# Ten more seven-product pairs in the second feed-forward, with their weight sums made in the mixers and kept in DRAM

## The chip, the cores and the metric

The kernel runs on one core of one Trainium2 chip. The metric is the device time in microseconds. The kernel before took 2288.7 us, the median of three runs (2288.67 to 2288.89).

## The reference

One layer of a decoder on 256 tokens of 2048 features, all in fp32: a gated feed-forward, two mixers of tokens side by side, a second gated feed-forward, and a gated embedding, each followed by a layer norm. Cut to what matters here:

```python
def swiglu(x, w_gu, w_down):
    g, u = jnp.split(x @ w_gu, 2, axis=-1)
    return (jax.nn.silu(g) * u) @ w_down

h = layer_norm(alpha * h + 0.5 * swiglu(h, w_ffn1_gu, w_ffn1_down), ...)   # f1
... # retention and sliding-window attention, gated, mixed                  # the mixers
h = layer_norm(alpha * h + mixed, ...)
h = layer_norm(alpha * h + 0.5 * swiglu(h, w_ffn2_gu, w_ffn2_down), ...)   # f2
ple = jax.nn.sigmoid(h @ w_ple_gate) * (p @ w_ple_proj)
h = layer_norm(alpha * h + ple, ...)
```

The change touches the product `x @ w_gu` of the second feed-forward: 256 x 2048 by 2048 x 11264.

## The kernel before

**Products.** Each fp32 operand is split into a high part (a copy to fp32r) and a low part (what the copy lost), and a product is three matmuls: low times high, high times high, high times low (`Sum.add`, lines 300 to 302). Weights come from HBM in chunks of 512 KB (`Chunk`, 128 partitions x 2 x 512 elements); for each, ACT makes the high part (`split`, line 93) and DVE the low one (line 94).

**Blocks.** The gate-and-up product of a feed-forward is done in eleven blocks (`for j in range(KF // 4)` in `ffn`), each of 512 columns of the gate and 512 of the up part. A block goes through eight pairs of 128-row slices of the weights, in an order written out as a string (`gu_units`, line 724). A letter P is a plain pair: two units `Single`, one for the gate and one for the up chunk, with 2 slices x 2 halves of the tokens x 3 = 12 matmuls each, 24 in all. A letter S is a `Seven` (line 142): Strassen's scheme, in Winograd's form, for the 2 x 2 block product of (two halves of the tokens, two slices) by (two slices, gate and up). It takes seven products for eight, 21 matmuls, and needs sums: of the activations (`seven_forms`, line 364, made once per feed-forward), and of the weights. For each seven DVE makes the four weight sums t1 to t4 (lines 165 to 168) in two tiles `u` and `v` of 128 x 1024, ACT and DVE split both, and they split the raw chunks too, as far as they are used. Block 0 has plain pairs alone; odd blocks have three sevens (`PPSPSPSP`, slices' pairs 0 to 2), even ones four (`PPSSPSSP`, pairs 0 to 3). At the end of a block's last seven, `seven_common` (line 401) and lines 825 to 830 join the sums; two units into the next block PE transposes the result (line 776).

**Order.** The program is written in the order in which each engine takes its instructions; an engine waits only for data and for room. Weight units stand in one list, `plan`, for the whole kernel. After each unit `done` calls `fill` (line 186): it issues the loads of further units on SP's queue while less than `far` (90) units of time are loaded or made, and has ACT and DVE split them while less than `ahead` (45) are made; a unit's time is 12 for a Single and 21 for a Seven, which is its matmuls. Both are held back by a budget, `slots_for_weights(n)`, of tiles of 4 KB a partition; a unit has `loads` (tiles that its load takes), `makes` (further ones while it is made) and `keeps` (those it holds until its matmuls are done). In f2 the budget is 24 from block 0 on. The tiles come from one pool of 46 (`SLOTS`), which holds activations too. A load whose tile is not free yet makes SP wait, with all that is queued behind it.

**Beside the matmuls.** `run_side` (line 236) is called after each unit. It takes one job from the list `side` (attention, transposes) and moves the first generator of the list `lazy` one step. The only generators are the tables of rotary angles, `rotary_table`: a DMA on ACT's queue, some twenty operations of 128 x 256 on DVE and two on ACT, in a dozen steps. The table for attention, "a", enters the list after the eight groups of queries and keys (`rqk`, until about 826 us), so it is made beside the three blocks of values (`rv`) that follow. After these come the retention's gates (`rg`), the attention's features (`av`, `aqk`), the two output gates (`gt`, `ga`), the output projections (`ma`, `mr`) and the mixing (`mo`). In the queries' and keys' stage, and at the attention's features, POOL multiplies by the angles (lines 931 to 933).

Of the kernel before, what the change touches and what calls it, by code (L numbers as in the profile page):

```python
# [8 lines left out]
F32 = mybir.dt.float32  # L9
F32R = mybir.dt.float32r  # L10
# [5 lines left out]
P = 128  # L16
# [20 lines left out]


SEVEN = (0, 1, 2, 3)

SEVEN_DOWN = (6, 7, 8, 9)

# [8 lines left out]
def layer(ctx: ExitStack, tc: tile.TileContext, io):  # L51
# [90 lines left out]
    class Seven:  # L142
# [12 lines left out]
        def make(self):  # L155
            a, b = self.a, self.b
            nm = a.name
            b11, b21, b12, b22 = a.of(a.raw, 0), a.of(a.raw, 1), b.of(b.raw, 0), b.of(b.raw, 1)
            u, v = (slot([P, 2, 512], F32, w + nm) for w in "uv")

            def shaped(x):
                return x.rearrange("p (g n) -> p g n", g=2) if a.paired else x

            t1, t3, t2, t4 = (shaped(x) for x in (u[:, 0], u[:, 1], v[:, 0], v[:, 1]))
            dve.tensor_tensor(t1, b11, b12, ALU.add)
            dve.tensor_tensor(t3, b12, b22, ALU.add)  # L166
            dve.tensor_tensor(t2, b11, t3, ALU.add)
# [12 lines left out]
            self.t1, self.t3 = parted("u", u)  # L180
            self.t2, self.t4 = parted("v", v)

    loaded, ready = [], []
    room = {"slots": 0, "used": 0, "ahead": 45, "far": 90, "quiet": False}
# [137 lines left out]
    def block_units(units, keys):  # L322

        for kind, p in units:
            if kind == "P":
                plan.extend(Single(keys(n, p)) for n in range(2))
            else:
                plan.append(Seven(keys(0, p), keys(1, p)))

    def block(name, units, keys, lhs, forms, sums, fold, before=None):  # L330


        sevens = [p for kind, p in units if kind == "S"]
        if sevens:
            p1, p6, p7, q5 = (Sum(bank(f"{name}s{j}"), len(sevens)) for j in range(4))
        for j, (kind, p) in enumerate(units):
            if before is not None:
                before(j)
            if kind == "P":
                for n in range(2):  # L340
                    u = take(keys(n, p))
                    tokens_chunk(u.chunk, 2 * p, lhs, [sums[t][n] for t in range(2)], (0, 1))
                    done(u)
                    run_side()
                continue
            u = take(keys(0, p))
            a11, a12 = (half_of(lhs(2 * p + e), 0) for e in range(2))
            a22 = half_of(lhs(2 * p + 1), 1)
            f5, f6, f7, f3 = forms(p)
            q2, q3, q4 = sums[0][0], sums[0][1], sums[1][0]  # L350
            steps = [
                (p1, a11, u.b11), (q2, a12, u.b21), (q3, f3, u.b22), (q5, f5, u.t1),
                (p7, f7, u.t3), (p6, f6, u.t2), (q4, a22, u.t4),
            ]
            if p == sevens[-1]:
                steps = [steps[j] for j in (0, 3, 5, 4, 1, 2, 6)]
            for to, left, right in steps:
# [32 lines left out]
    def units_of(order, sevens):  # L390

        sevens = list(sevens)
        plain = [p for p in range(KD // 2) if p not in sevens]
        return [(kind, (sevens if kind == "S" else plain).pop(0)) for kind in order]

    def block_sums(ps, units, n_k):

# [323 lines left out]
        yield  # L721


    def gu_units(j):
        if j == 0:
            return [("P", p) for p in range(KD // 2)]
        order = "PPSSPSSP" if j % 2 == 0 else "PPSPSPSP"
        return units_of(order, SEVEN[: order.count("S")])

# [19 lines left out]

    def plan_ffn(name):  # L750
        for j in range(KF // 4):
            block_units(gu_units(j), gu_keys(name, j))
        first, second, held = down_units(HELD_PAIRS[name == "f2"])
        block_units(first, down_keys(name, 0))
        block_units(second, down_keys(name, 1))
        plan.extend(Single(down_keys(name, 1)(n, p)) for n in range(2) for p in held)

    def ffn(name, i, ht, norm, keep, residual, keepers, away):
# [27 lines left out]

        for j in range(KF // 4):
            pg, pu = banks(f"{name}g{j}"), banks(f"{name}u{j}")
            units = gu_units(j)
            plain = len(units) - sum(kind == "S" for kind, p in units)  # L790
            n_of = {(0, 0): KD, (0, 1): KD, (1, 0): KD, (1, 1): KD}
            for kind, p in units:
                if kind == "S":
                    for at in ((0, 0), (0, 1), (1, 0)):
                        n_of[at] -= 1
                    n_of[1, 1] -= 2
            sums = [[Sum((pg, pu)[n][t], n_of[t, n]) for n in range(2)] for t in range(2)]
            got = []

            if norm is not None and j == 0:  # L800
                front, units = units[:FRONT_PAIRS], units[FRONT_PAIRS:]
                steps = [(gu_keys(name, 0)(n, p), 2 * p, n) for _, p in front for n in range(2)]
                norm.first(steps, rhs, sums, (
                    (3, (1, 0)), (5, (1, 1)), (7, (0, 2)), (8, (1, 2)), (9, (0, 3)), (10, (1, 3)), (10, "go"),
                ))
                slots_for_weights(24)

            def before(u, j=j, offset=KD // 2 - len(units)):
                u += offset
                if j == 0 and norm is None and u % 2 == 0:  # L810
                    first_chunk(u // 2)
                    if u == 6:
                        slots_for_weights(24)
                    if u == 2:
                        load_constants()
                if j == 0 and u == 7:
                    for g in sorted({p // 2 for p in SEVEN}):
                        hi, lo = (slot([P, 8, P], F32R, f"{name}f{w}{g}") for w in "hl")
                        made[g] = seven_forms(keep[g], hi, lo)
                if j == KF // 4 - 1 and u in (4, 6):  # L820
                    convert(u // 2 - 2)

            block(f"{name}{j}", units, gu_keys(name, j), rhs, forms, sums, lambda *a: got.extend(seven_common(*a)), before)
            if got:
                g, v = got
                for x, ps in ((g, pg), (v, pu)):
                    for t in range(2):
                        dve.tensor_tensor(x[:, t], x[:, t], ps[t], ALU.add)  # L828
                act.activation(g, g, AF.Silu)  # L829
# [141 lines left out]
    def mixers(ht, norm, residual, keepers, away):  # L971
# [27 lines left out]
            done(u)  # L999
        values(0, ps)  # L1000
        slots_for_weights(14)
        for grp in range(8):
            ps = banks(f"rqk{grp}")
            features_out([(("w_in_f", grp), ps)], KD, both_halves)
            rotated(grp, ps)
        grp = 8
        decay = [slot([P, 2, 384], F32, f"dec{j}") for j in range(4)]
        for j in range(4):
            act.dma_start(decay[j], io["decay"][:, 2 * j : 2 * j + 2, :])
        lazy.append(rotary_table("a"))  # L1010
        for blk in range(1, 4):
            ps = banks(f"rv{blk}")
            tokens_out(("w_rv", blk), KD, rhs, ps)
# [290 lines left out]

        lhs = lambda k: of_pairs(mix_t, k)
        slots_for_weights(16)
        for blk in range(3):
            if blk == 2:
                load_for_norm(1)
            ps = banks(f"mo{blk}")  # L1310
            y[blk] = load_columns(residual, blk, "mixy")
            tokens_out(("w_mix", blk), KD, lhs, ps)
            for t in range(2):
                dve.scalar_tensor_tensor(y[blk][:, t], y[blk][:, t], ALPHA, ps[t], ALU.mult, ALU.add)
            block_stats(stats, y, blk)
# [307 lines left out]
```

## Time and profile before

| | |
|---|---|
| Median of three runs | 2288.7 us |
| The profiled execution's own time | 2289.47 us |
| Its span, first to last instruction | 2287.7 us |
| Mean granted TensorE clock | 0.999 |
| DVE, busy share of the span | 85% |
| ACT, busy share of the span | 52% |
| DMA traffic | 465.88 MB, 204 GB/s on average |
| HBM read, written | 455.60 MB, 8.39 MB |

The kernel's stages by the trace: f1's gate and up to about 520 us, its second product to 690, the mixers to 1480, f2's gate and up to 1956, its second product to 2155, then the embedding. A stretch of the windows view gives its length and then, for PE, PEld (weight loads), DVE, ACT and POOL, the busy time with the number of instructions, and last the granted clock, the DMAs' busy share and GB/s. A line of the tile view gives the smallest, median and largest duration of an instruction in ns, the first and last start, and the shape. Busy time of PE overlaps from one matmul to the next, so the length of a stretch divided by its matmuls tells more than a matmul's duration.

### The profile page before, as it was taken

To read this page: it belongs to the slowest core of one execution; us is meant where nothing else is said; L and a number is where in the kernel's file an instruction comes from. 1 tells how busy PE (TensorE), PEld (TensorE's weight loads), DVE (VectorE), ACT (ScalarE), POOL (GpSimd) and SP (SyncE) were. 2 spreads that over 40 slices of the span, in tenths; PEclk is the share of its full clock that TensorE was granted. 3 is DMA by queue.
4 is the path that set the end of the run, shared out by engine and by line. 5 is a ranking of instruction groups with operands and counts; after the bars stand their busy time and mean duration, and the time that the engine had idled before them with its cause. 6 is when DMAs were issued, how large, how long until landed. Compare 5 with 4: busy or idle time off the path is not lost.

```text
span 2287.7 us, 28860 instructions
## 1 busy us (share of the span) xinstructions
PE 2271.4 (99%) x10490; PEld 1884.8 (82%) x10490; DVE 1947.8 (85%) x2474; ACT 1190.0 (52%) x1438; POOL 97.0 (4%) x56
## 2 busy tenths in 40 slices
PE   9999999999999999999999999999999999999998
PEld 7888888888888888888778888888888888888876
DVE  7899999999988785677789786779999999889877
ACT  6555555556554342435556454355565555555533
POOL 0000000000000530124000000000000000000000
PEclk9999999999999999999999999999999999999999
DMA  8666665655677565555447567566666566565772
GB/s 298 202 204 199 197 210 180 207 198 191 217 278 279 178 221 167 167 165 165 139 149 244 168 222 275 192 233 205 195 191 205 184 203 214 181 221 193 276 258 74
DMA packets 194022, 465.88 MB, mean 204 GB/s; under 512 B 14796, under 2 KB 16460, under 8 KB 193880
## 3 DMA queue, kind: packets, MB, share of 16 engines
q1 hardware_dynamic: 191752, 461.20, 61.0%
q10 hardware_dynamic: 2128, 2.84, 0.4%
q8 instruction: 82, 1.34, 0.2%
q14 instruction: 60, 0.49, 0.1%
HBM read 455.60 MB, written 8.39 MB: 203 GB/s over the span
## 4 chain that ended last, share of the span: by engine, by line
PE 95%; DVE 3%; DMA 1%; issue 0%; ACT 0%; DVEq 0%; ACTq 0%
PE f1g L300 3%; PE f1g L301 3%; PE f1g L302 3%; PE f2g L302 3%; PE f2g L300 3%; PE f2g L301 3%; PE rqk L251 3%; PE f1u L302 2%; PE f1u L301 2%; PE f1u L300 2%; PE f2u L302 2%; PE f2u L300 2%; PE f2u L301 2%; PE aqk L251 2%; PE f1d L300 2%; PE f2d L301 2%
## 5 line engine op out<-in xcount | busy, mean ns | idle before, releaser
L94 DVE TENSOR_TENSOR lf_gu<-rf_gu,hf_gu 128x1024 fp32r<-128x1024 f32 (+1 forms) x284 | 334.3, 1210 | 15.1 <-ACT hf_gu L93 14.3
L93 ACT CAST hf_gu<-rf_gu 128x1024 fp32r<-128x1024 f32 (+1 forms) x284 | 282.3, 1043 | 19.6 <-DMA rf_gu<-in_f_gu 19.4
L94 DVE TENSOR_TENSOR lw_in_f<-rw_in_f,hw_in_f 128x1024 fp32r<-128x1024 f32 x140 | 195.6, 1427 | 29.5 <-ACT hw_in_f L93 26.9
L94 DVE TENSOR_TENSOR lf_down<-rf_down,hf_down 128x1024 fp32r<-128x1024 f32 x152 | 181.1, 1219 | 22.7 <-ACT hf_down L93 20.2
L93 ACT CAST hf_down<-rf_down 128x1024 fp32r<-128x1024 f32 x152 | 155.2, 1050 | 74.8 <-DMA rf_down<-in_f_down 21.2
L93 ACT CAST huf_gu<-uf_gu 128x1024 fp32r<-128x1024 f32 x70 | 73.7, 1053 | 157.8 <-DVE uf_gu L166 155.2
L93 ACT CAST hw_in_f<-rw_in_f 128x1024 fp32r<-128x1024 f32 x140 | 138.9, 1051 | 2.2 <-DMA rw_in_f<-in_w_in_f 1.1
L300 PE MATMUL f1g<-hf_gu,xt 128*128 128x512 f32 x247 | 97.0, 393 | 0.8 <-ACT hf_gu L93 0.8
L301 PE MATMUL f1g<-hf_gu,xt 128*128 128x512 f32 x247 | 96.8, 392 | 0.0
L302 PE MATMUL f1g<-lf_gu,xt 128*128 128x512 f32 x247 | 96.7, 391 | 0.0
L300 PE MATMUL f2g<-hf_gu,ht 128*128 128x512 f32 x247 | 96.3, 390 | 0.0
L302 PE MATMUL f2g<-lf_gu,ht 128*128 128x512 f32 x247 | 96.2, 389 | 0.0
L301 PE MATMUL f2g<-hf_gu,ht 128*128 128x512 f32 x247 | 96.1, 389 | 0.0
L93 ACT CAST hvf_gu<-vf_gu 128x1024 fp32r<-128x1024 f32 x70 | 73.8, 1054 | 29.7 <-DVE vf_gu L168 29.4
L829 ACT ACTIVATE eve<-eve 128x1024 f32<-128x1024 f32 x20 | 21.2, 1061 | 124.4 <-DVE eve L828 124.4
L94 DVE TENSOR_TENSOR luf_gu<-uf_gu,huf_gu 128x1024 fp32r<-128x1024 f32 x70 | 85.2, 1217 | 0.0
L94 DVE TENSOR_TENSOR lvf_gu<-vf_gu,hvf_gu 128x1024 fp32r<-128x1024 f32 x70 | 85.2, 1217 | 0.0
L300 PE MATMUL f2u<-hf_gu,ht 128*128 128x512 f32 x212 | 83.8, 395 | 0.0
L300 PE MATMUL f1u<-hf_gu,xt 128*128 128x512 f32 x212 | 83.4, 393 | 0.0
L302 PE MATMUL f2u<-lf_gu,ht 128*128 128x512 f32 x212 | 82.6, 390 | 0.0
L301 PE MATMUL f2u<-hf_gu,ht 128*128 128x512 f32 x212 | 82.6, 390 | 0.0
L301 PE MATMUL f1u<-hf_gu,xt 128*128 128x512 f32 x212 | 82.6, 389 | 0.0
(1358 smaller groups left out, 6446.2 us busy)
## 6 DMA issues: line engine op xcount, KB each, us to landing
rf_gu<-in_f_gu SPq DMA_DIRECT2D x350, 512.0 KB
rf_down<-in_f_down SPq DMA_DIRECT2D x176, 512.0 KB
rw_in_f<-in_w_in_f SPq DMA_DIRECT2D x148, 512.0 KB
rw_rv<-in_w_rv SPq DMA_DIRECT2D x32, 512.0 KB
rw_ret<-in_w_ret SPq DMA_DIRECT2D x32, 512.0 KB
rw_mix<-in_w_mix SPq DMA_DIRECT2D x32, 512.0 KB
rw_pg<-in_w_pg SPq DMA_DIRECT2D x32, 512.0 KB
rw_att<-in_w_att SPq DMA_DIRECT2D x16, 512.0 KB
```

Of the source, the lines that this page charges most:

```text
L93: act.copy(dst_hi, src)
L94: (lo_engine or dve).tensor_tensor(dst_lo, src, dst_hi, ALU.subtract)
L251: pe.matmul(ps[f], hi[:, kk, f * P : (f + 1) * P], rhs(k), start=k == 0, stop=k == n_k - 1,)
L300: pe.matmul(o, al, bh, start=first, stop=False)
L301: pe.matmul(o, ah, bh, start=False, stop=False)
L302: pe.matmul(o, ah, bl, start=False, stop=self.left == 0)
L829: act.activation(g, g, AF.Silu)
```

## The change

In f2's blocks 1, 3, 5, 7 and 9 two plain pairs (pairs 4 and 5) become units of a new kind, D (`Prepared`): the order is `PPSDSDSP`. A D unit does the same seven products, and its four weight sums are not made on the spot. Its load brings the gate chunk (512 KB), that half of the up chunk which is used by itself (256 KB), and the high and low parts of `u` and `v` (four times 512 KB) from DRAM, six loads in all; the making of it splits the first two alone.

The sums and their parts are made in the mixers by `sums_ahead`, a generator of the list `lazy`. For each of the ten pairs it loads the two raw chunks, adds and splits, and stores the four parts in DRAM, 2 MB, in four pieces with pauses of `every` steps between them. Three pairs are made at a pause of 2, three at 3 and two at 5, from the values' blocks on; the last two, at 2, in the mixing. The next pair's raw chunks are loaded in the middle of a pair. The table of the attention's angles moves ahead of the queries' and keys' groups.

In f2's block 0 the sums of activations for pairs 4 and 5 are made as well (`forms_of`: one add of 128 x 1024, four of 128 x 256, one split). The budget of tiles becomes 32 - j at the start of each of the five blocks (31, 29, 27, 25, 23), and stays so in the block after it.

```diff
+AHEAD = (4, 5)
+AHEAD_BLOCKS = (1, 3, 5, 7, 9)
+AHEAD_SLOTS = 32
...
+    class Prepared:
+        loads, makes, keeps, time = 6, 3, 7, 21
...
+        def load(self):
+            self.a = Chunk(self.key)
+            self.b = slot([P, 2, 256], F32, "r" + self.a.name + "b")
+            sync.dma_start(self.b, chunk_of(self.other)[:, :, 256:])
+            self.sums = []
+            for w, v in zip(("hu", "lu", "hv", "lv"), put_by_sums.pop(self.key)):
+                t = slot([P, 2, 512], F32R, w + self.a.name)
+                sync.dma_start(t.bitcast(F32), v)
+                self.sums.append(t)
+
+        def make(self):
+            a = self.a
+            a.make()
+            self.b11, self.b21 = a.columns(0), a.columns(1)
+            both = slot([P, 2, 512], F32R, "b" + a.name)
+            self.b22 = both[:, 0], both[:, 1]
+            split(*(both[:, e].rearrange("p (g n) -> p g n", g=2) for e in range(2)), self.b)
...
+    def sums_ahead(items, wait, every):
...
+        pairs = [[Chunk(k) for k in items[0]]]
+        for _ in range(wait):
+            yield
+        for j, (key, _) in enumerate(items):
...
+            dve.tensor_tensor(t1, b11, b12, ALU.add)
+            dve.tensor_tensor(t3, b12, b22, ALU.add)
+            act.copy(uh, u)
+            yield from pause()
+            dve.tensor_tensor(t2, b11, t3, ALU.add)
+            dve.tensor_tensor(t4, t2, b21, ALU.add)
+            act.copy(vh, v)
+            if j + 1 < len(items):
+                pairs.append([Chunk(k) for k in items[j + 1]])
+            yield from pause()
+            dve.tensor_tensor(ul, u, uh, ALU.subtract)
+            yield from pause()
+            dve.tensor_tensor(vl, v, vh, ALU.subtract)
+            for e in range(2):
+                sync.dma_start(away[e], parts[e].bitcast(F32))
+            yield from pause()
+            for e in range(2, 4):
+                sync.dma_start(away[e], parts[e].bitcast(F32))
...
-    def gu_units(j):
+    def gu_units(name, j):
         if j == 0:
             return [("P", p) for p in range(KD // 2)]
+        if name == "f2" and j in AHEAD_BLOCKS:
+            return units_of("PPSDSDSP", SEVEN[:3], AHEAD)
...
                         made[g] = seven_forms(keep[g], hi, lo)
+                    if name == "f2":
+                        g = AHEAD[0] // 2
+                        made[g] = forms_of([ht[:, 4 * g : 4 * g + 4, :]], f"{name}f{g}")
+                if name == "f2" and j in AHEAD_BLOCKS and u == 0:
+                    slots_for_weights(AHEAD_SLOTS - j)
...
         slots_for_weights(14)
+        lazy.append(rotary_table("a"))
         for grp in range(8):
...
-        lazy.append(rotary_table("a"))
+        ahead = [(gu_keys("f2", j)(0, p), gu_keys("f2", j)(1, p)) for j in AHEAD_BLOCKS for p in AHEAD]
+        for items, every in ((ahead[:3], 2), (ahead[3:6], 3), (ahead[6:8], 5)):
+            lazy.append(sums_ahead(items, 3, every))
         for blk in range(1, 4):
...
         slots_for_weights(16)
+        lazy.append(sums_ahead(ahead[8:], 4, 2))
         for blk in range(3):
```

More of the change, by code (lines that the diff above doesn't have):

```diff
@@ L181, in make, with __init__ @@
             self.t2, self.t4 = parted("v", v)
+    put_by_sums = {}
+    class Prepared:
+        loads, makes, keeps, time = 6, 3, 7, 21
+        def __init__(self, key, other):
+            self.key, self.other = key, other
+        def load(self):
[14 more added lines that the diff above has]
+            split(*(both[:, e].rearrange("p (g n) -> p g n", g=2) for e in range(2)), self.b)
+            uh, ul, vh, vl = self.sums
+            self.t1, self.t3 = ((uh[:, e], ul[:, e]) for e in range(2))
+            self.t2, self.t4 = ((vh[:, e], vl[:, e]) for e in range(2))
@@ new lines, in sums_ahead, with pause @@
+    def sums_ahead(items, wait, every):
+        def pause():
+            for _ in range(every):
+                yield
+        pairs = [[Chunk(k) for k in items[0]]]
+        for _ in range(wait):
+            yield
+        for j, (key, _) in enumerate(items):
+            a, b = pairs.pop()
+            b11, b21, b12, b22 = a.of(a.raw, 0), a.of(a.raw, 1), b.of(b.raw, 0), b.of(b.raw, 1)
+            u, v = (slot([P, 2, 512], F32, w + a.name) for w in "uv")
+            t1, t3, t2, t4 = (x.rearrange("p (g n) -> p g n", g=2) for x in (u[:, 0], u[:, 1], v[:, 0], v[:, 1]))
+            parts = [slot([P, 2, 512], F32R, w + a.name) for w in ("hu", "lu", "hv", "lv")]
+            uh, ul, vh, vl = parts
+            away = [dram.tile([P, 2, 512], F32, name=f"{w}{a.name}") for w in ("hud", "lud", "hvd", "lvd")]
+            put_by_sums[key] = away
+            dve.tensor_tensor(t1, b11, b12, ALU.add)
[16 more added lines that the diff above has]
+                sync.dma_start(away[e], parts[e].bitcast(F32))
@@ L327, in block_units @@
             else:
-                plan.append(Seven(keys(0, p), keys(1, p)))
+                plan.append((Seven if kind == "S" else Prepared)(keys(0, p), keys(1, p)))
     def block(name, units, keys, lhs, forms, sums, fold, before=None):
-        sevens = [p for kind, p in units if kind == "S"]
+        sevens = [p for kind, p in units if kind != "P"]
         if sevens:
@@ L388, in forms_of, with units_of @@
         return seven_forms(whole(parts, name + "w"), hi, lo)
[L390 to L394, printed above, removed]
+    def units_of(order, sevens, ahead=()):
+        sevens, ahead = list(sevens), list(ahead)
+        plain = [p for p in range(KD // 2) if p not in sevens + ahead]
+        of = {"S": sevens, "D": ahead, "P": plain}
+        return [(kind, of[kind].pop(0)) for kind in order]
     def block_sums(ps, units, n_k):
@@ L751, in plan_ffn @@
         for j in range(KF // 4):
-            block_units(gu_units(j), gu_keys(name, j))
+            block_units(gu_units(name, j), gu_keys(name, j))
         first, second, held = down_units(HELD_PAIRS[name == "f2"])
@@ L788, in ffn @@
             pg, pu = banks(f"{name}g{j}"), banks(f"{name}u{j}")
-            units = gu_units(j)
-            plain = len(units) - sum(kind == "S" for kind, p in units)
+            units = gu_units(name, j)
             n_of = {(0, 0): KD, (0, 1): KD, (1, 0): KD, (1, 1): KD}
             for kind, p in units:
-                if kind == "S":
+                if kind != "P":
                     for at in ((0, 0), (0, 1), (1, 0)):
```

## The prediction, made before the changed kernel was run

> **What bounds the kernel now.** I read the page first, then the windows that end at a block's transposes (line 776) in the second feed-forward, then the waits of PE, the waits of SP's queue, and last the DMA rates in stretches of 10 us. Engine lines: busy us, share, count.
>
> ```profile
> span 2287.7 us, 28860 instructions
> PE 2271.4 (99%) x10490; PEld 1884.8 (82%) x10490; DVE 1947.8 (85%) x2474; ACT 1190.0 (52%) x1438; POOL 97.0 (4%) x56
> ...
> q1 hardware_dynamic: 191752, 461.20, 61.0%
> ...
> PE 95%; DVE 3%; DMA 1%; issue 0%; ACT 0%; DVEq 0%; ACTq 0%
> ```
>
> PE is 95% of the chain that ended last; it is full, so time goes only where matmuls go or where a new wait stops PE. Between 1480 and 2150 us PE's list of waits holds one entry, of 0.3 us. The four windows run from the transposes of block 0 to those of block 4 (blocks 1 to 4):
>
> ```profile
> 1535.57:1577.95 42.38, 42.38 (x193) 35.17 (x192) 36.40 (x43) 23.43 (x27) 0.00 (x0) 1.00 0.62 199
> 1577.95:1619.65 41.70, 41.70 (x191) 34.63 (x189) 41.11 (x50) 23.97 (x27) 0.00 (x0) 1.00 0.57 190
> 1619.65:1662.02 42.37, 42.37 (x193) 35.19 (x192) 38.22 (x44) 23.44 (x27) 0.00 (x0) 1.00 0.63 199
> 1662.02:1703.71 41.69, 41.69 (x190) 34.61 (x189) 41.17 (x50) 23.98 (x27) 0.00 (x0) 1.00 0.59 187
> ```
>
> PE fills each to the hundredth. Odd blocks have three sevens (8 pairs x 24 matmuls - 3 x 3 = 183), even ones four (180). The difference, 0.68 us, is three matmuls: 0.227 us each; (42.38 - 0.87 for the eight transposes) / 183 gives 0.2268. DVE is busy 41.1 of 41.7 us in an even block: a fifth seven made on the spot would not fit there. That is the limit that the change goes around.
>
> **Part 1, PE.** In blocks 1, 3, 5, 7 and 9 two plain pairs (24 matmuls each) become D units (21). 10 x 3 x 0.2267 = **6.80 us less**; an odd block should take 42.38 - 6 x 0.2267 = 41.02 us. No matmul is added.
>
> **Part 2, sums in the mixers.** The costs come from the rows of this work as it is done now:
>
> ```profile
> L94 DVE TENSOR_TENSOR lf_gu<-rf_gu,hf_gu x135: 1214/1217/1226, 1499.0 to 1939.4; 128x1024 fp32r<-128x1024 f32 x135
> L93 ACT CAST hf_gu<-rf_gu x133: 1034/1047/1068, 1499.8 to 1936.3; 128x1024 fp32r<-128x1024 f32 x133
> L93 ACT CAST bf_gu<-rf_gu x35: 609/616/635, 1526.1 to 1929.7; 128x512 fp32r<-128x512 f32 x35
> L165 DVE TENSOR_TENSOR uf_gu<-rf_gu,rf_gu x35: 678/684/687, 1528.1 to 1931.5; 128x512 f32<-128x512 f32 x35
> L167 DVE TENSOR_TENSOR vf_gu<-rf_gu,uf_gu x35: 691/692/695, 1529.4 to 1932.9; 128x512 f32<-128x512 f32 x35
> L94 DVE TENSOR_TENSOR bf_gu<-rf_gu,bf_gu x35: 681/684/689, 1531.9 to 1935.4; 128x512 fp32r<-128x512 f32 x35
> ```
>
> An item is four adds (2 x 0.684 + 2 x 0.692) and two subtractions (2 x 1.217): 5.2 us of DVE, 2.1 us of ACT. What stands free there (us, PE, PEld, DVE, ACT, POOL):
>
> ```profile
> 737.00:826.00 89.00, 89.00 (x512) 78.39 (x511) 70.02 (x62) 33.22 (x46) 45.21 (x21) 1.00 0.56 178
> 826.00:892.00 66.00, 66.00 (x292) 54.66 (x292) 38.91 (x52) 26.82 (x31) 5.70 (x3) 1.00 0.72 233
> 892.00:995.00 103.00, 103.00 (x483) 86.16 (x482) 72.40 (x153) 41.07 (x53) 10.97 (x6) 1.00 0.53 166
> 995.00:1067.00 72.00, 72.00 (x446) 63.90 (x445) 54.27 (x101) 30.94 (x56) 26.44 (x14) 1.00 0.49 153
> 1067.00:1173.00 106.00, 106.00 (x539) 83.23 (x539) 78.07 (x147) 60.03 (x125) 6.58 (x4) 1.00 0.48 148
> 1385.00:1466.00 81.00, 81.00 (x367) 67.05 (x366) 55.17 (x57) 36.36 (x39) 0.00 (x0) 1.00 0.68 230
> ```
>
> By the steps of `run_side` (one a chunk) three items fall in the first 28 chunks after 826 us, three in the next 40, two in the 44 after that (they end with the gates, near 1173), two in the 21 from 1385. From 826 to 1173 DVE is idle 103 us against 8 x 5.2 = 42; from 1385 to 1466 it is idle 26 against 10. A piece is at most two adds (1.4 us), and DVE's low parts are ready 5 to 12 us ahead of PE in most of these stages (3.8 at worst, at 838 us, amid the rotary table's 20 small operations, which the change takes away from there). So PE should not see it: cost 0, bounds -1 (that table gone) to +5. Queues passed: 20 loads and 40 stores more on SP, 0.4 us of issue each; a store waits for a subtraction issued one pause, 2 to 5 chunks, earlier, and SP, which runs ahead of the plan where slots are free, falls back to about the plan's 19 us ahead of PE, against 3.4 us from issue to last packet of a lone 512 KB load in the trace. Slots: the pool of 46 has 11 or more free wherever an item (5 to 10 slots) is alive, at least 6 after it.
>
> The table for the attention's angles moves into 737 to 826 us: 7.1 us of DVE there against 19 us idle. There the low part `lw_in_f` takes a median of 2.31 us where it takes 1.22 elsewhere, and POOL is busy 45 of the 89 us. The Trainium skill (SBUF — State Buffer, Who interferes with whom) has a DVE instruction with two SBUF inputs and a GpSimd one that reads SBUF exclude each other for the whole instruction. By that rule, which the trace's doubled row agrees with, the table could take up to 14 us, still under 19; taken as a price on PE it would be 0 by the one and by the other.
>
> **Part 3, block 0 of the second feed-forward.** One more `forms_of`: a 128x1024 add (1.22), four 128x256 (0.42 each), a subtraction (1.22), 4.1 us of DVE. DVE is idle 4.16 us just there (1522.7 to 1526.8). First use is by the first D unit, 22 us on. Cost 0, bounds 0 to 1.
>
> **Part 4, the odd blocks.** A D unit costs DVE 1.22 + 0.68 = 1.9 us where the pair cost 2.4, ACT 1.66 where it cost 2.1: relief, worth nothing while PE is the bound. What grows is DMA. A chunk is 512 KB = 0.524 MB; a D unit loads 0.524 + 0.262 + 4 x 0.524 = 2.88 MB where the pair loaded 1.05. An odd block goes from 8.39 to 12.06 MB: 294 GB/s over 41.0 us, 247 over an odd and an even block (20.45 MB in 82.7 us). What can the DMAs give? 461.2 MB at 61.0% of 2287.7 us is 330 GB/s when busy. Full stretches (last two columns: DMA share, GB/s):
>
> ```profile
> 12.00:22.00 10.00, 10.00 (x46) 8.29 (x45) 8.57 (x8) 7.60 (x8) 0.00 (x0) 1.00 1.05 388
> 22.00:32.00 10.00, 10.00 (x46) 8.29 (x45) 6.96 (x6) 5.49 (x6) 0.00 (x0) 1.00 0.94 299
> 835.00:845.00 10.00, 10.00 (x46) 8.29 (x45) 9.69 (x19) 1.06 (x1) 0.00 (x0) 1.00 1.01 408
> ```
>
> So 299 to 408; I take 330. Then come the slots. I counted by `fill`'s rules when each load is issued and which freed slot it takes (the oldest freed first). Today loads of these blocks have 20 to 31 us to their use so counted, and the trace shows 25 to 44. With the change, blocks 1 and 3 keep 19 to 29. In blocks 5, 7 and 9 the budget (27, 25, 23 slots) holds back the second D unit and the last seven: 63 matmuls, 14.3 us, to their use.
>
> For those blocks, from the D unit's issue: first packet 1.0 us (as in that lone load), 2.88 MB at 330 is 8.7, landed at 9.7; use at 14.3. The last seven's loads may start at 4.8 but land behind, at 9.7 + 3.2 = 12.9; its use is at 19.0. Making a seven takes 6.75 us on DVE from first add to last part (1571.76 to 1578.51): done at 19.6, and the last part is read only by the ninth matmul, at 20.8. That leaves 1.2 us, and the limit is (20.8 - 6.75 - 1.0) for 3.93 MB: 301 GB/s. It holds at 330, barely not at 299. I take 0.2 us a block, **0.6 us** in all; bounds 0 to 8 (2.7 a block at 250 GB/s).
>
> **The sum.** The profiled execution took 2289.47 us, span 2287.7 and 1.8 around it, 0.8 above the median of 2288.7. 2289.47 - 6.80 + 0.6 = 2283.3 on that execution; on the median **2282.5**.
>
> **Rivals.** (a) Late loads in blocks 5, 7 and 9. For it: a margin of 1.2 us and 299 GB/s in one full stretch; against it: 388 and 408 in others. At 270 GB/s, 1.5 us a block, the time is 2286.4; it may reach 2290. (b) A wait in the mixers: ACT and DVE take their work in order, so an add whose raw pair has not landed, or a copy that waits for it, holds up the weight parts queued behind, and PE once the lead is used. For it: 3.8 us of lead at 838 and 5 near 1162; against it: three or more chunks (8 us) between load and add. Ten items at 0.3 to 0.5 us past the lead: 2285 to 2287. (c) **Slower**: the DMAs cannot feed an odd and an even block in 82.7 us. This begins at 247 GB/s and has eaten the gain at 243; at 233 a pair of blocks takes 87.8 us, five of them add 25 us, and the time is 2307. For it: the most that two slices of the page (114 us) moved is 279, and the parts come back from a place in DRAM that nothing has read so far; against it: the full stretches above, and that the parts' rows of 4 KB should go in packets of 4 KB, which take 0.159 us where one of 2 KB takes 0.084. (d) The matmuls do not go: PE's count would stay at 10490, and the time at 2288.7 or above. The code leaves no room for it.
>
> **How the numbers follow.** The measurement can tell about 0.2%, 4.6 us, from no change: faster is under 2284.1. The forecast (new waits under 2.2 us) 0.70; (a) 0.12 and (b) 0.08, both mostly within 0.2%; (c), with anything like it, 0.10. The range goes from 2281.0 (all of the 6.8 us and 0.9 for part 2's lower bound) to 2288.0, which holds the forecast and most of (a) and (b).
>
> **What would show it.** PE's count 10460; the odd windows 41.0 us and the even ones unchanged; DMA bytes up by 10 x (1.05 read and 2.10 written in the mixers, 1.84 in the blocks) = 50 MB to 516; DVE up some 52 us between 826 and 1466. Wrong would be: PE idle in blocks 5, 7 and 9 before the second D unit or the last seven; PE waiting for low parts between 826 and 1173; an odd window over 42.4.

## The result, and the profile after

The changed kernel took **2300.41 us**, the median of four runs (2298.26 to 2301.51), against 2288.74 for the kernel before. The ratio of the runs is 1.0046 (95% interval 1.0034 to 1.0059), that of the two medians 1.0051. It is slower by 11.7 us, where 6.2 us less was forecast. The profiled execution took 2299.85 us, with a span of 2298.1.

The page of the changed kernel, the same rows that the prediction showed of before:

```profile
span 2298.1 us, 29122 instructions
...
PE 2270.9 (99%) x10460; PEld 1880.4 (82%) x10460; DVE 2000.8 (87%) x2540; ACT 1207.7 (53%) x1459; POOL 94.2 (4%) x56
...
q1 hardware_dynamic: 208712, 511.02, 65.6%
...
PE 84%; DVE 10%; issue 2%; ACT 2%; DMA 1%; DVEq 0%; SPq 0%; ACTq 0%
```

The matmuls went (10490 to 10460), and DVE has 53 us more. What is new stands in the last row: PE was 95% of the chain that ended last and is 84% now; DVE's share grew from 3% to 10%, and ACT and "issue" have 2% each.

The windows of the second feed-forward, blocks 1, 2, 9 and 10 (length, then PE, PEld, DVE, ACT, POOL):

```profile
1551.30:1592.33 41.03, 41.03 (x187) 34.06 (x186) 36.53 (x44) 22.26 (x26) 0.00 (x0) 1.00 0.71 228
1592.33:1634.02 41.69, 41.69 (x190) 34.63 (x189) 41.17 (x50) 24.50 (x28) 0.00 (x0) 1.00 0.77 266
...
1881.40:1922.75 41.35, 41.33 (x186) 34.00 (x186) 34.73 (x42) 20.71 (x26) 0.00 (x0) 1.00 0.71 252
1922.75:1966.20 43.45, 42.27 (x189) 34.42 (x188) 42.86 (x49) 26.83 (x31) 0.00 (x0) 1.00 0.72 229
```

Block 1 takes 41.03 us, where 41.02 was worked out, and block 2 is as before. Block 9 takes 0.3 us more than block 1, and block 10 takes 43.45 where every even block took 41.69 before; PE is not full in it and DVE is busy for nearly all of it. The mean granted clock was 0.997, where it was 0.999 before; since the stretches that PE fills are as long as before (41.69 us for an even block), the clock is not where the time went.

The first matmul of each stage, after less before, tells where the rest went:

| stretch, by PE's first matmul in each | after less before |
|---|---|
| up to the queries and keys (736 us) | 0.0 us |
| values, retention gates, attention features (736 to 1045) | +7.8 |
| attention, output gates (1045 to 1173) | +6.7 |
| gates' blocks, projections, mixing (1173 to 1385) | 0.0 |
| mixing's end, norm, block 0 (1385 to 1535) | +1.5 |
| blocks 1 to 8 | -5.4 |
| block 9 | -1.05 (41.33 for 42.37) |
| block 10 | +1.76 |
| second product, norm, embedding | -1.4 |

The sum is +9.8 us. The gain is all there; **14.5 us are lost in the mixers**, where PE never waited before. Its waits there now, by what ended them (us in total, times, the longest), name 9.6 of the 14.5:

```profile
PE ro L1122 <- DVE rsc L1112: 4.6, 3, 2.1
PE at L1277 <- DVE asc L1267: 4.2, 3, 1.8
PE at L1277 <- ACT hw_in_f L98: 0.8, 1, 0.8
```

PE waits for the scores of retention (`rsc`) and of attention (`asc`), jobs that go from PE to DVE or ACT and back, and not for sums of weights. The same stretch (890 to 1190 us) in ACT's list of waits has two rows at its top that the kernel before does not have:

```profile
ACT huf_gu L240 <- DVE uf_gu L239: 34.7, 4, 14.4
ACT hvf_gu L244 <- DVE vf_gu L243: 23.3, 5, 9.0
```

These are the two copies in `sums_ahead`, each written right behind the adds whose result it copies. Here is one of them in ACT's order of time, and DVE's row behind it (start, us, instruction, idle before and who ended it):

```profile
901.69 1.05 ACT L98 CAST hw_in_f<-rw_in_f 128x1024 fp32r<-128x1024 f32 x1 [2.03 <-DVE lw_in_f L99]
917.14 1.05 ACT L240 CAST huf_gu<-uf_gu 128x1024 fp32r<-128x1024 f32 x1 [14.40 <-DVE uf_gu L239]
```

```profile
915.76 0.69 DVE L238 TENSOR_TENSOR uf_gu<-rf_gu,rf_gu 128x512 f32<-128x512 f32 x1
...
920.14 4.86 DVE L99 TENSOR_TENSOR lw_in_f<-rw_in_f,hw_in_f 128x1024 fp32r<-128x1024 f32 x3 [3.09 <-ACT hw_in_f L98]
```

ACT had come to the copy at 902.7, and DVE made the adds at 915.8: ACT works that far ahead of DVE (before, at 898 us, up to 27 us ahead of PE where DVE is some 10). While it stands, it makes none of the high parts that DVE will need next. So DVE, done with the adds at 917.1, waits 3.1 us for the next high part.

The length of the wait is not its cost. Before, ACT stood even longer at this place, for PE's retention gates, and PE lost nothing by it. What the copy changes is when the work behind it in ACT's queue can start. Here are the gates before, and after:

```profile
915.93 1.28 ACT L1103 ACTIVATE rgs<-rg 128x512 f32<-128x512 f32 x2 [17.60 <-PE rg L302]
```

```profile
918.09 1.08 ACT L1187 ACTIVATE rgs<-rg 128x512 f32<-128x512 f32 x2
```

They start 2.2 us later, and the next high part 2.0 us later (919.06 for 917.10). At the next copy into `huf_gu`, which waits 11.28 us, the retention's `rett` behind it starts at 959.18 for 954.68. So the high parts and the jobs of the mixers that pass through both engines come late, by a little more at each copy.

### The profile page after: what moved, and what is told of

It reads as the page before. It is cut to its first block, busy times and chain, and to the rows that moved or that the text cites. A ratio compares the mean times of both kernels' runs of the same rounds, so it can differ in the third digit from the quotient of the medians.

```text
span 2298.1 us, 29122 instructions
## 1 busy us (share of the span) xinstructions
PE 2270.9 (99%) x10460; PEld 1880.4 (82%) x10460; DVE 2000.8 (87%) x2540; ACT 1207.7 (53%) x1459; POOL 94.2 (4%) x56
## 4 chain that ended last, share of the span: by engine, by line
PE 84%; DVE 10%; issue 2%; ACT 2%; DMA 1%; DVEq 0%; SPq 0%; ACTq 0%
PE f1g L374 3%; PE f1g L375 3%; PE f1g L376 3%; PE rqk L325 3%; PE f1u L376 2%; PE f1u L374 2%; PE f1u L375 2%; PE f2g L376 2%; PE f2g L375 2%; PE f2g L374 2%; DVE lw_in_f L99 2%; PE f2u L375 2%; PE f2u L374 2%; PE f2u L376 2%; PE f2d L374 2%
## 5 line engine op out<-in xcount | busy, mean ns | idle before, releaser
L99 DVE TENSOR_TENSOR lf_gu<-rf_gu,hf_gu 128x1024 fp32r<-128x1024 f32 (+1 forms) x274 | 322.8, 1211 | 14.4 <-ACT hf_gu L98 13.6
L98 ACT CAST hf_gu<-rf_gu 128x1024 fp32r<-128x1024 f32 (+1 forms) x274 | 273.7, 1043 | 34.1 <-DMA rf_gu<-in_f_gu 32.5
L374 PE MATMUL f2g<-hf_gu,ht 128*128 128x512 f32 x217 | 84.7, 390 | 0.0
L376 PE MATMUL f2g<-lf_gu,ht 128*128 128x512 f32 x217 | 84.5, 390 | 0.0
L375 PE MATMUL f2g<-hf_gu,ht 128*128 128x512 f32 x217 | 84.5, 389 | 0.0
L376 PE MATMUL f1u<-lf_gu,xt 128*128 128x512 f32 x212 | 82.6, 390 | 0.0
L374 PE MATMUL f2u<-hf_gu,ht 128*128 128x512 f32 x172 | 68.2, 397 | 0.0
L376 PE MATMUL f2u<-lf_gu,ht 128*128 128x512 f32 x172 | 67.1, 390 | 0.0
```

The lines of the kernel that those rows point to most:

```text
L98: act.copy(dst_hi, src)
L99: (lo_engine or dve).tensor_tensor(dst_lo, src, dst_hi, ALU.subtract)
L374: pe.matmul(o, al, bh, start=first, stop=False)
L375: pe.matmul(o, ah, bh, start=False, stop=False)
L376: pe.matmul(o, ah, bl, start=False, stop=self.left == 0)
```

## The experiments

**Theory 1**: the copies make ACT wait for DVE, ACT loses its lead, and DVE then waits for ACT. **Rivals**: (2) DVE's 42 us of new work is itself too much there; (3) the stores, which wait in SP's queue, and the traffic make the weights late; (4) the blocks' loads cost what part 4 feared. Three sets of four kernels ran, each set beside the kernel before on one chip. The profiled executions begin up to 1.5 us apart, so the table at the end of this section counts from the queries and keys on.

**The blocks alone.** No sums are made in the mixers; the D units load other rows of the same size in place of the parts, so the result is of other data.

```diff
-            for w, v in zip(("hu", "lu", "hv", "lv"), put_by_sums.pop(self.key)):
+            for w, v in zip(("hu", "lu", "hv", "lv"), rows[0]):
...
-        for items, every in ((ahead[:3], 2), (ahead[3:6], 3), (ahead[6:8], 5)):
-            lazy.append(sums_ahead(items, 3, every))
...
-        lazy.append(sums_ahead(ahead[8:], 4, 2))
```

> Leaves out the sums in the mixers; the D units load four stored tiles of the first residual in the parts' place (same sizes, same rows), so the product is not the reference's. The traces put 14.4 us of loss between the retention's gates and the gates' stage, 1.5 at the norm after the mixing, 1.8 in block 10, and 6.8 of gain in the odd blocks. If the loss is the mixers' alone, the time is 2288.7 - 6.8 + 0.4 = 2282 to 2283 us. If the odd blocks themselves cost block 10 its 1.8 us, 2283 to 2284. If late loads in the blocks mattered (rival a or c), above 2286.

Measured: 2283.75 us, ratio 0.9974 (0.9965 to 0.9983), some 5.3 us less. The mixers cost nothing (0.0), blocks 1 to 8 give their 5.4 us, and blocks 9 and 10 lose 2.8 against 82.7, with no sums made anywhere: that loss belongs to the blocks.

**The mixers alone.** Sums made and stored, the second feed-forward as before.

```diff
-        if name == "f2" and j in AHEAD_BLOCKS:
+        if False:
             return units_of("PPSDSDSP", SEVEN[:3], AHEAD)
...
-                    if name == "f2":
-                        g = AHEAD[0] // 2
-                        made[g] = forms_of([ht[:, 4 * g : 4 * g + 4, :]], f"{name}f{g}")
-                if name == "f2" and j in AHEAD_BLOCKS and u == 0:
-                    slots_for_weights(AHEAD_SLOTS - j)
```

> Makes and stores the sums in the mixers, and leaves the second feed-forward as it was, so nothing reads them. If the mixers' loss stands by itself: 2288.7 + 14.4 + 1.5 = 2303 to 2306 us. If the loss came from the blocks: 2289 to 2291.

Measured: 2305.5 us, ratio 1.007 (1.0055 to 1.0086), +16.4 us: 14.5 in the mixers and 1.1 in the norm, where the change has 14.5 and 1.5. As far as these numbers go, the two halves do not depend on each other.

**Copies that do not wait.** ACT copies the raw chunk in place of the sum: the same instruction, with nothing to wait for. The "high part" is then another number than the sum's, and the low part makes up the rest.

```diff
-            act.copy(uh, u)
+            act.copy(uh, a.raw)
...
-            act.copy(vh, v)
+            act.copy(vh, b.raw)
```

> ACT's two copies in each item take the raw chunks in place of the sums (so the parts are wrong); ACT, DVE, loads and stores do as much as before, but ACT no longer waits for DVE's adds. Theory 1 (the copy makes ACT wait up to 14 us, its lead over DVE goes, and DVE then waits for each cast): most of the mixers' 14.4 us goes, 2286 to 2290 us. Theory 2 (DVE's 42 us of added work between 826 and 1188 us makes the retention's and attention's jobs late): 2297 to 2301. Theory 3 (stores and raw loads hold up SP and the weights): 2297 to 2301.

Measured: 2290.66 us, ratio 1.0007 (0.9997 to 1.0016). The mixers lose 2.0 us and not 14.5. DVE's work and the stores are all still there, so (2) and (3) are not what costs most.

**Copies one pause later.** The sums' own high parts again, but each copy is written after the next pause, two to five chunks on.

```diff
-            act.copy(uh, u)
             yield from pause()
+            act.copy(uh, u)
...
-            act.copy(vh, v)
             if j + 1 < len(items):
                 pairs.append([Chunk(k) for k in items[j + 1]])
             yield from pause()
+            act.copy(vh, v)
```

> The same work and the reference's result; each of ACT's copies is issued one pause (2, 3 or 5 chunks) after the adds that it reads. Theory 1: ACT's wait shrinks by 5 to 14 us each, and the time falls to 2286 to 2292 us. Theories 2 and 3: 2297 to 2301.

Measured: 2291.37 us, ratio 1.001 (1.0 to 1.0019). The mixers lose 3.0 us: 0.1 up to the attention (7.8 in the change) and 2.8 beside attention and gates (6.7). Of the copies' waits in ACT's list, 58.0 us in nine times in the change, one of 7.5 us is left, and DVE's waits for ACT's high parts between 890 and 1178 us, 35.1 us in 22 times in the change, are below the kernel before's 26.9:

```profile
DVE lw_in_f L99 <- ACT hw_in_f L98: 15.9, 14, 1.8
```

**Theory 1 is shown**: two lines moved, and 11.5 us are back. Three losses are left: 2.8 us beside the gates, 3.5 in the norm (1.5 in the change), 2.5 in blocks 9 and 10. All kernels that follow keep this edit; the first four take the losses one by one.

**No stores.** The stores are left out, and the D units load other rows, so the result is of other data.

```diff
-            for e in range(2):
-                sync.dma_start(away[e], parts[e].bitcast(F32))
             yield from pause()
-            for e in range(2, 4):
-                sync.dma_start(away[e], parts[e].bitcast(F32))
```

> Edit: the copies one pause later, as in the run before it that took 2291.4 us, and the forty stores of finished parts are left out (the blocks then load four tiles of the activations' rows of the same size instead, so the data is not the sums; the bytes read are the same). In that earlier run the first product of the feed-forward starts 7.0 us late: 3.0 us of it before the gate stage, 0.5 at its end, 3.5 in the norm after the mixing. Theory S (the stores wait in SP's queue for VectorE and put off the loads behind them, which then come in a crowd at the norm): the 3.5 us go, 2287.9 us, and the 3.0 us stay, since they are VectorE's own work beside the attention. Theory V (VectorE's 13 us of adds and subtractions stand ahead of the norm): both stay, 2291.4 us. If the stores are behind both: about 2285 us.

Measured: 2287.64 us, ratio 0.9994 (0.9985 to 1.0004). The norm's loss is 0.0; the 2.7 us beside the gates stay. So the norm pays for the stores, and the gates for something else.

**More budget.**

```diff
-AHEAD_SLOTS = 32
+AHEAD_SLOTS = 36
```

> Edit: the copies one pause later, and the slots for weights in the odd blocks start at 36 rather than 32, so that block 9 has 27 of them and not 23. Block 9's last group of seven has raw weights that land late; its window was 41.7 us and block 10's 43.5, where 41.0 and 41.7 stand in the other pairs: 2.5 us. Theory B (the loads are late since the slots are short): the 2.5 us go, 2288.9 us. Theory D (VectorE is full in the pair of blocks, or the DMA engines are): 2291.4 us as before. If the ring of slots is too short for 27 beside the finished activations, slots are waited for and the time is over 2292 us.

Measured: 2292.24 us, ratio 1.0015 (1.0006 to 1.0024). Blocks 9 and 10 lose 2.8 us as before: not the budget, then. (The norm lost 5.9 here with the same code ahead of block 1; that loss is between 1.1 and 5.9 us in the runs that have it.)

**Six pairs.** Only blocks 1, 3 and 5; nothing beside the gates, nothing in the mixing.

```diff
-AHEAD_BLOCKS = (1, 3, 5, 7, 9)
+AHEAD_BLOCKS = (1, 3, 5)
...
-        for items, every in ((ahead[:3], 2), (ahead[3:6], 3), (ahead[6:8], 5)):
+        for items, every in ((ahead[:3], 2), (ahead[3:6], 3)):
...
-        lazy.append(sums_ahead(ahead[8:], 4, 2))
```

> Edit: the copies one pause later; only blocks 1, 3 and 5 take two groups each, so six groups are summed in the mixers, all while the values and the first attention products run; none beside the gating and none in the mixing. Three odd blocks save 1.36 us each: 4.1. Theory P (what was left of the loss depends on the place: items seven and eight beside the gating, items nine and ten before the norm, block 9's loads): nothing else is lost, 2289.1 - 4.1 = 2285.0 us, plus 0 to 0.5. Theory N (each item costs the same, some 0.65 us of PE's time in the mixers): 6 x 0.65 = 3.9 us lost, 2288.9 us.

Measured: 2284.66 us, ratio 0.9981 (0.9972 to 0.9991). The mixers lose 0.1 us. Six pairs' sums, 31 us of DVE, cost nothing where they stand, so there is no fixed price for a pair. That the place decides is shown by the kernels with eight pairs below.

**Eight pairs.** Blocks 1, 3, 5 and 7, the seventh and eighth pair beside the gates, none in the mixing.

```diff
-AHEAD_BLOCKS = (1, 3, 5, 7, 9)
+AHEAD_BLOCKS = (1, 3, 5, 7)
...
-        lazy.append(sums_ahead(ahead[8:], 4, 2))
```

> Edit: the copies one pause later; blocks 1, 3, 5 and 7 take two groups each, eight groups are summed, none of them in the mixing. Four odd blocks save 5.4 us. Theory P (the norm loses only by the items put into the mixing, and blocks 9 and 10 only by block 9's own loads): the mixers' 3.0 us are lost, 2289.1 - 5.4 + 3.0 = 2286.7 us. If the norm still loses 3.5 us without items in the mixing, 2290.2 us; if blocks 9 and 10 still lose 2.5 us, 2289.2 us.

Measured: 2285.85 us, ratio 0.999 (0.998 to 0.9999). The 2.8 us beside the gates are back, the norm and blocks 9 and 10 lose nothing. PE's waits between 1075 and 1178 us, a list that is empty with six pairs:

```profile
PE at L1277 <- DVE asc L1267: 1.4, 1, 1.4
PE at L1277 <- ACT hw_in_f L98: 0.7, 1, 0.7
```

The scores of attention again: by these waits the chain from PE over DVE and ACT back to PE has no room here for two pairs' sums, though DVE is idle 27.5 us of the 100 from 1075 with six pairs. POOL may have a part in it: at 1076.88 us the pair's subtraction `luf_gu` took 2.30 us and the low part behind it 2.31, where each takes 1.22 elsewhere, beside POOL's work on the angles (L1013 and L1014). No run separates the two.

**Two tiles more.** With more budget, block 9 had the budget but the ring of 46 tiles was the same. Here the D units use the activations' forms of an earlier group, so that two tiles of the ring stay free; the result is of other activations.

```diff
-                        made[g] = forms_of([ht[:, 4 * g : 4 * g + 4, :]], f"{name}f{g}")
+                        made[g] = made[1]
```

> Edit: the copies one pause later (2291.4 us alone), and the ten groups multiply with the activations' forms that the second pair of units already has, not with forms of their own: two slots of the ring stay free through all blocks, some six instructions in block 0 go, and the result is that of other activations. In the kernel with the copies late VectorE waits 5.9 us in block 9 for a slot that PE gives back, and blocks 9 and 10 lose 0.7 and 1.8 us. More budget with the same ring gave nothing back. Theory R (the ring of 46 slots itself is short in block 9): with two slots free block 9 stands as block 7 stood, whose lateness cost nothing; the 2.5 us go to 0.5 or less, 2288.9 to 2289.4 us. Theory D (VectorE's own work fills blocks 9 and 10): 2291.4 us.

Measured: 2289.59 us, ratio 1.0004 (0.9995 to 1.0013). The windows of blocks 9 and 10:

```profile
1873.80:1914.81 41.01, 41.01 (x186) 34.05 (x185) 36.51 (x45) 22.29 (x26) 0.00 (x0) 1.00 0.74 258
1914.81:1956.50 41.69, 41.69 (x189) 34.61 (x188) 41.10 (x47) 25.03 (x28) 0.00 (x0) 1.00 0.72 240
```

All 2.5 us are back. (The norm lost 4.8 here.) In the kernel with the late copies DVE has one wait in block 9, ahead of the first sum of a seven; the list puts it down to a matmul that gives a tile back. DVE's lost time comes out a block later, since block 10 has no room on DVE:

```profile
DVE uf_gu L170 <- PE f2g L376: 5.9, 1, 5.9
```

In the change the same sum waits 6.0 us, in the blocks alone 6.8, and with more budget 6.9, each time for the load of its raw chunk. With the two tiles free it still waits 3.9 us for that load, and this much costs nothing.

**Two pairs beside the projections.** Six pairs as above, the seventh and eighth in the stage from 1255 to 1385 us, blocks 1, 3, 5 and 7.

```diff
         slots_for_weights(20)
+        lazy.append(sums_ahead(ahead[6:], 3, 3))
         for j in range(4):
             v = sig[4 + j]
```

> Edit: the copies one pause later; six groups summed in the values and the first attention products, two more beside the attention output product and the two retention output blocks (the stage from 1255 to 1385 us of the kernel before, where VectorE had 30 of 130 us idle), none beside the gating, none in the mixing; blocks 1, 3, 5 and 7 take two each. Theory P (a place costs by what it does to the chain PE - VectorE - ScalarE - PE there, and no such chain runs in this stage): nothing is lost, 2289.0 - 5.4 = 2283.6 us. Theory S (the stores wait in SP's queue and put off loads here as they did before the norm): 1 to 3.5 us lost, 2284.6 to 2287 us.

Measured: **2282.65 us**, ratio 0.9973 (0.9962 to 0.9984), the lowest of all (the intervals of the blocks alone and of the last kernel overlap with this one's). Nothing is lost in the mixers (0.2 us in all) or in the norm. Its page, and that stage's window:

```profile
PE 2265.5 (99%) x10466; PEld 1878.9 (82%) x10466; DVE 1989.0 (87%) x2528; ACT 1205.4 (53%) x1455; POOL 94.7 (4%) x56
...
PE 95%; DVE 3%; DMA 1%; issue 0%; ACT 0%; DVEq 0%; ACTq 0%
```

```profile
1254.40:1384.10 129.70, 129.70 (x581) 107.43 (x580) 109.64 (x125) 67.82 (x73) 0.00 (x0) 1.00 0.76 260
```

The chain is PE's at 95% again. DVE's 99.9 us of the kernel before have become 109.6, two pairs' sums, and the stage takes 129.70 us in both. The stores were SP's here, and cost nothing: it is not SP's stores as such that cost.

**The mixing's stores on GpSimd's queue.** All ten pairs, late copies.

```diff
-                sync.dma_start(away[e], parts[e].bitcast(F32))
+                (queue or sync).dma_start(away[e], parts[e].bitcast(F32))
...
-        lazy.append(sums_ahead(ahead[8:], 4, 2))
+        lazy.append(sums_ahead(ahead[8:], 4, 2, pool))
```

> Edit: the copies one pause later; all ten groups as in the change, but the stores of the two groups summed in the mixing are issued by GpSimd's queue, which has nothing else to do there, rather than by SP. Nothing is left out. Theory S (SP's stores put off the loads of the mixing and of block 0): the norm's 3.5 us go as they did without any stores, 2291.4 - 3.5 = 2287.9 us. Theory T (the stores' traffic itself, 4 MB in all, crowds the loads): 2291.4 us, some of it at most back.

Measured: 2287.55 us, ratio 0.9992 (0.9983 to 1.0001). The norm loses 0.0, with the same bytes stored. So it is the wait of the store in SP's queue, not the traffic. The same wait by the lists of SP's queue between 1385 and 1490 us: with SP's stores and late copies it holds the row

```profile
SPq L252 <- DVE luf_gu L248: 11.5, 2, 8.3
```

and with GpSimd's no such row. The loads behind it are those of the mixing's last chunks and of block 0. SP starts on ten loads of block 0 at 1457.47 us with its own stores and at 1454.13 with GpSimd's. With its own, DVE stands for those weights just ahead of the norm, makes the sum that leads into the norm (`mixy`, L1387) at 1474.65 rather than 1470.68, and PE waits for it (of both differences 0.4 us was there before this stage; waits of 1440 to 1500 us):

```profile
DVE lf_gu L99 <- ACT hf_gu L98: 3.5, 2, 2.1
...
PE lnps L593 <- DVE mixy L586: 3.4, 3, 2.6
```

With GpSimd's stores the first row is not there and the second is 0.3 us. In the change itself the DMA engines are full just ahead of the norm (before: 0.48 and 161 GB/s in the same 40 us):

```profile
1440.00:1480.00 40.00, 40.00 (x178) 33.12 (x178) 32.27 (x34) 22.22 (x23) 0.00 (x0) 1.00 0.99 383
```

With the late copies the same 40 us show 0.77 and 280 GB/s, and the norm loses more (3.5 us for 1.5), so it is not shown that full DMA engines cost anything there.

**Eight pairs, the last two in the mixing, stored by GpSimd.**

```diff
-AHEAD_BLOCKS = (1, 3, 5, 7, 9)
+AHEAD_BLOCKS = (1, 3, 5, 7)
...
-        for items, every in ((ahead[:3], 2), (ahead[3:6], 3), (ahead[6:8], 5)):
+        for items, every in ((ahead[:3], 2), (ahead[3:6], 3)):
...
-        lazy.append(sums_ahead(ahead[8:], 4, 2))
+        lazy.append(sums_ahead(ahead[6:], 4, 2, pool))
```

> Edit: the copies one pause later; six groups in the values and the first attention products with SP's stores, two in the mixing with GpSimd's stores, none beside the gating; blocks 1, 3, 5 and 7 take two each. If the theories hold together (copies cost ScalarE its lead; items beside the gating cost 2.8 us; SP's stores cost the norm 3.5; block 9's slots cost 2.5), nothing is lost: 2289.0 - 5.4 = 2283.6 us, faster than the six groups' 2284.7. If the stores' traffic and not SP's queue is what the norm pays for, 3 us more: 2286.6 us.

Measured: 2283.83 us, ratio 0.9976 (0.9967 to 0.9985). With all four causes out of the way the blocks' gain is left, less 0.5 us in the norm.

All runs, in us against the kernel before's profiled execution, counted from the queries and keys on (mixers: to the gates' blocks; norm: from the mixing to block 1; last: second product to the embedding's norm):

| kernel | mixers | norm | blocks 1-8 | 9 and 10 | last |
|---|---|---|---|---|---|
| the change | +14.5 | +1.5 | -5.4 | +0.7 | -1.4 |
| blocks alone | 0.0 | 0.0 | -5.4 | +1.4 | -0.8 |
| mixers alone | +14.5 | +1.1 | 0 | 0 | +0.4 |
| copies of raw | +2.0 | +2.9 | -5.4 | +0.5 | -1.3 |
| copies late (in all below) | +3.0 | +3.5 | -5.4 | +1.1 | -1.3 |
| no stores | +2.8 | 0.0 | -5.4 | +0.7 | -0.7 |
| more budget | +2.9 | +5.9 | -5.4 | +1.4 | -1.2 |
| six pairs | +0.1 | +0.1 | -4.1 | 0 | -1.1 |
| eight pairs | +2.9 | 0.0 | -5.4 | 0 | -0.6 |
| two tiles more | +3.0 | +4.8 | -5.4 | -1.4 | -1.5 |
| two beside projections | +0.2 | 0.0 | -5.4 | 0 | -0.9 |
| GpSimd's stores | +3.0 | 0.0 | -5.4 | +1.1 | -0.7 |
| eight, GpSimd's stores | +0.2 | +0.5 | -5.4 | 0 | +0.2 |

## Why the prediction was wrong

**Part 1 held.** 30 matmuls fewer; the odd windows are 41.03 and 41.01 us where 41.02 was worked out; 5.44 us in blocks 1 to 8.

**Part 2 is the step that failed**: "So PE should not see it: cost 0, bounds -1 (that table gone) to +5". It cost 14.5 us in the mixers. The argument was a share: DVE is idle 103 us in that stretch, the work is 42, and DVE is 5 to 12 us ahead of PE. With the copies placed otherwise, 31 us of the same work did cost nothing. What was not asked is what ACT does at the copy: in the kernel before it was ahead of DVE by as much as 17 us (27.6 ahead of PE, where DVE was 10.1, for the chunk made at 897 us), and it takes its work in order. The prediction read DVE's lead over PE, but not ACT's lead over DVE. Rival (b) named this mechanism ("a copy that waits for it holds up the weight parts queued behind") and priced it at 0.3 to 0.5 us an item past the lead. Over the eight items of this stretch it was 1.4 us an item (11.5 of the 14.5 us came back with two lines moved), since each copy lets what stands behind it in ACT's queue start late too: the gates by 2.2 us at the first one shown, `rett` by 4.5 at the next.

Two smaller parts of the same step failed as well. For the stores it counted on subtractions made well ahead and on SP's 19 us of lead over PE; SP reaches a store before DVE has made the part, and stood 14.0 us in two waits for `luf_gu` in the mixing. That costs 1.5 us here, 1.1 to 5.9 in all runs that have it. And the two items beside the gates cost 2.8 us with the copies late: PE waits there for the attention's scores, whose chain has less room than DVE's idle time says.

**Part 3** put block 0's forms at 0 by DVE's time, which was right for DVE. Their two tiles were the cost: with two free, blocks 9 and 10 lose nothing.

**Part 4** forecast 0.6 us, in blocks 5, 7 and 9, by the bandwidth. It was 0 in 5 and 7 and 2.1 in 9 and 10 together. The bandwidth was ample: these blocks moved 214 to 266 GB/s with the DMA engines busy 0.66 to 0.77. Held back were the loads, as the prediction said, but by the ring of 46 tiles and not by the budget that it counted (9 and 10 lose 2.8 with 27 slots in place of 23). The margin was also taken at PE's use in the same block. The time that DVE lost there was paid in block 10: DVE did 1.8 us less in block 9 (34.7 for the 36.5 of the kernel with two tiles more), and block 10 has 41.1 us of DVE's work of its own in 41.7.

**The moved table** cost nothing, as forecast: the retention's gates begin at 890.61 us, 0.03 earlier than before. Rivals (c) and (d) did not come; the slower result has another cause.

**The end** gave back 1.4 us: PE's waits for DVE at the second feed-forward's norm fall from 1.4 to 0.2 us, and a wait of 1.3 at the embedding is gone. No run tests why. The medians differ by 11.7 us and the two profiled executions by 10.4; the four runs of the changed kernel are up to 3.3 us apart, and those of the kernel before, beside the first set of experiments, up to 5.1.

## What to carry to other kernels

Before work is put into an engine's idle time, ask for each instruction which engine it waits for and how far its own engine is ahead of that one: an in-order engine that runs ahead and is made to wait for a slower one loses its lead, and all that lives on that lead is late. How long it waits says little (17.6 us of waiting cost nothing before); what stands behind the waiting instruction says more. Two lines moved by one pause were worth 11.5 us of 14.5. Then look at the place (a chain that passes through several engines has less room than any one of them shows), at what the instruction holds up in its queue, stores too, and at the tiles it keeps until the end.

## What the hardware showed

Two things were not expected. Three small operations of DVE with one tensor as input were stretched beside POOL. The first is the multiplication at the end of the table of angles, before (at 849 us, POOL idle since 833) and after its move (POOL multiplying from 760.39 to 762.50 and again until 763.79):

```profile
L714 DVE TENSOR_SCALAR triga<-rota,cst x1: 345/345/345, 849.4 to 849.4; 128x256 f32<-128x256 f32 x1
```

```profile
L789 DVE TENSOR_SCALAR triga<-rota,cst x1: 1378/1378/1378, 761.3 to 761.3; 128x256 f32<-128x256 f32 x1
```

0.35 us became 1.38. It ends at 762.65, 0.15 us after POOL's instruction, and the next two (0.28 and 0.29 us before) took 1.38 and 1.32 in the same way. The Trainium skill (SBUF — State Buffer, Who interferes with whom) has the one that comes second wait for the whole instruction of the other, also for a `tensor_scalar` in a mode that uses both ports; the times agree with that, though no trace shows the mode itself. The lesson for the sum is that the doubled `lw_in_f` is not the only row that POOL touches.

And the DMA engines moved 383 GB/s for 40 us on end in the change, with a share of 0.99, where the prediction reckoned with 330 and had seen 388 and 408 for 10 us only.
